# Two more gated channel pairs by seven block products, and the recurrence's chunks regrouped

## The chip, the cores and the metric

One core of a Trainium2 chip runs the whole program. The metric is the device time of one execution in microseconds (us); three runs of the kernel before have a median of 1548.71 us. TensorE (PE) multiplies matrices, ScalarE (ACT) applies functions and copies, VectorE (DVE) does elementwise arithmetic and scans, GpSimd (POOL) and SyncE (SP) mainly start transfers (DMA). Each engine works through its own instructions in the order in which the program lists them; between engines only semaphores order the work.

## What is computed

A decoder layer on `x` of 1024 positions by 1024 channels, all in float32:

```python
h = rms_norm(x, g_mix)
z = einsum("bsd,de->bse", h, w_in) + b_in
va, ga, xb, gb, sa, sb = split(z, cuts)      # 1024, 1024, 1536, 1536, 1024, 1024 channels
u = causal_depthwise_conv(va * sigmoid(ga), conv_a_w, conv_a_b)     # 31 taps
y_a = silu(layer_norm(u, ln_g, ln_b)) @ w_a_out
v = causal_depthwise_conv(xb, conv_b_w, conv_b_b)                   # 4 taps
r, i = sigmoid(block_diag(v, w_a) + b_a), sigmoid(block_diag(v, w_x) + b_x)   # 16 heads
a = exp(-8 * r * softplus(-lam))
hidden = scan(a, sqrt(1 - a*a) * i * v)      # linear recurrence over positions
y_b = (hidden * gelu(gb)) @ w_b_out
x = x + (sigmoid(sa) * y_a + sigmoid(sb) * y_b) @ w_o
x = x + square(relu(rms_norm(x, g_mlp) @ w_1)) @ w_2
out = rms_norm(x, g_final)
```

## The kernel before, in words

**Precision.** Every float32 operand is split into a high and a low part; a product is three matmuls (high by high, high by low, low by high). One matmul is a 128x128 weight block by 128x512.

**Columns of z.** They are numbered in chunks of 128 channels: VA 0 to 7, GA 8 to 15, XB 16 to 27, GB 28 to 39, SA 40 to 47, SB 48 to 55.

**First part** (the loop over `s`, one chunk a slot, order in the list `CH`). A chunk is 24 weight blocks by two halves of 512 positions, 48 matmuls (`chunk_mm`, line 735). The first part computes all of VA, GA and XB, 28 chunks. A VA/GA pair becomes `u = va*sigmoid(ga)` (`u_out`), and DVE runs the 31 taps on it (`conv`, lines 630 to 655, one filter of 48 instructions for each j). These taps are filler: a planner with a clock for each engine (`clk`, `later`, `vector_work`, `fill`) puts them between DVE's other work at build time. An XB chunk gets its four taps (`xb_out`) and is split (`xb_parts`); three XB chunks make a group of four heads. A head's two gates share one PSUM region of two banks (`ps2`, a single buffer): `head_mm(n, 0)` ends slot HS0[n], `head_gate(n, 0)` (a sigmoid on ACT, line 542) empties it, `head_mm(n, 1)` follows in the next slot behind 18 of the chunk's 24 blocks, `head_gate(n, 1)` empties it, and then comes `head_mm(n+1, 0)`. HS0 begins the four groups at slots 4, 9, 14 and 19, so that one slot without a new head lies between two groups. In the slot behind a group's last head comes `scan_exp` (three exp and three tanh on ACT), later `scan_root` (three square roots, line 564; `lag` puts it one slot further for the first three groups) and `scan_tile` for each of the group's three chunks (DVE, lines 573 to 576).

On ACT a slot's order is: `head_gate(before, 0)`, `xb_out` or `u_out`, `w_parts` (weights of the next chunk, two instructions), `head_gate(before, 1)`, `xb_parts`, `head_w_parts`, then `scan_exp` and `scan_root`. ACT holds one set of functions at a time; sigmoid, exp/tanh, and square root come with an ACT_TABLE_LOAD between them in the trace.

**Second part** (the loop over `zseq`). GB, SA and SB are computed by pairs of chunks: the weights as 2x2 blocks (two chunks by two halves of the 1024 input channels), the activations as 2x2 blocks (two halves of the channels by two halves of the positions), seven block products of 12 matmuls each (`z_mm`, line 933) in place of eight. `zseq` lists the products as (pair, p). Products 1, 2 and 3 take blocks of h as they are; 4 to 7 take sums and differences of them, which `x_load`, `x_sum` and `x_parts` prepare at the end of the first part and the start of the second. At step n of the loop: ACT copies or evacuates what product n-1 left (`z_post`), PE runs product n, ACT and POOL split the weight operand of product n+4 (`z_lhs`: either two ACT instructions with an accumulating POOL transfer between, or ACT and DVE), DVE makes the weight sums of product n+5 (`z_sums`), and SP starts loads listed in `ZL`. Product 1 of a pair fills PSUM bank a; `z_post` copies a to bank b, product 2 goes on accumulating in a, product 6 in b; b is copied to e and to a buffer u, product 7 fills f. A bank that no matmul has written before is first opened by one throwaway matmul (`z_bank`, line 922).

**After that** come the branch outputs (from line 1121), the layer norm of the filtered branch (it needs `ysum`, the sum of all eight filters' results), the output projection, and the MLP, all on PE.

The activation pool (`T`) has 37 tiles of 128x1024.

Of the kernel before, what the change touches and what calls it, by code (L numbers as in the profile page):

```python
# [9 lines left out]
F32 = mybir.dt.float32  # L10
# [3 lines left out]
ALU = mybir.AluOpType  # L14

P = 128
# [15 lines left out]
def trunk_kernel(ctx: ExitStack, tc: tile.TileContext, x, xt_in, xt_eo, vecs, w_in, w_a_out, w_b_out,  # L32
# [636 lines left out]
    def x_load(c2):  # L669

        xq[c2] = {n: ep.tile([P, S], F32, tag="e", name=f"xs{n}_{c2}") if (n, c2) == (21, 0) else T(f"xs{n}_{c2}")
                  for n in (11, 12, 22, 21)}
        for n, a in xq[c2].items():
            nc.sync.dma_start(a, xu[n % 10 - 1, 2 * (n // 10 - 1) + c2])
# [18 lines left out]

    CH = [XB, VA, GA, XB + 1, XB + 2]
    for js, g in (((1,), 1), ((2,), 2), ((3,), 3), ((4, 5, 6, 7), 4)):
        CH += [c for j in js for c in (VA + j, GA + j)]
        CH += [XB + t for t in range(3 * g, min(3 * g + 3, 12))]
    NC1 = len(CH)
# [39 lines left out]

    ZPAIRS = [GB + 2 * i for i in range(6)] + [SA + 2 * i for i in range(4)]
    ZPAIRS += [SB + 2 * i for i in range(4)]  # L740
    NZ = len(ZPAIRS)
# [3 lines left out]
    def z_load(i, kk):  # L745

        zraw[i, kk] = raw = qp.tile([P, 2, 4, P], F32, tag="p", name=f"zw{i}_{kk}", bufs=4)
        c = ZPAIRS[i]
        nc.sync.dma_start(raw, w_in[c:c + 2, :, 4 * kk:4 * kk + 4, :].rearrange("m p k c -> p m k c"))

# [18 lines left out]
    def z_lhs(i, p):  # L769
        src = z_blk(i, *{1: (0, 0), 2: (0, 1), 4: (1, 1)}[p]) if p in (1, 2, 4) else \  # L770
            zs[i, {3: 4, 5: 1, 6: 2, 7: 3}[p]]
# [12 lines left out]

    zseq = [(0, 1), (1, 1), (0, 2), (1, 2), (0, 6), (0, 7), (1, 7), (0, 5), (1, 6), (0, 3), (0, 4),
            (1, 5)]
    for i in range(2, NZ):
        zseq += [(i, 1), (i, 7), (i - 1, 4), (i, 6), (i, 2), (i - 1, 3), (i, 5)]
    zseq[-7:] = [(NZ - 1, p) for p in (1, 7, 6)] + [(NZ - 2, 4), (NZ - 1, 2), (NZ - 1, 5), (NZ - 2, 3)]
# [3 lines left out]
    for i in range(2, NZ):  # L793
        n = zseq.index((i, 1))
        ZL[n - 9] = ((z_load, i, 0),)
        ZL[n - (6 if i > 2 else 4)] = ((z_load, i, 1),)
    def z_get(n, f):
# [3 lines left out]
               mybir.EngineType.SP, mybir.EngineType.Pool}  # L801
    HS0 = [4 + 5 * (n // 4) + n % 4 for n in range(NH)]
    head_at = {s: n for n, s in enumerate(HS0)}

    EXP = {head_slot: g for g, head_slot in enumerate(HS0[4 * g + 3] + 1 for g in range(4))}
    XL = {23: 0, 25: 1}
    XS = {25: ((x_parts, 0, 6),), 26: ((x_parts, 0, 7, 5),), 27: ((x_parts, 0, 4),)}
    w_load(3)
# [5 lines left out]
    with tc.manual_schedule(engines=ENGINES):  # L814
        for s in range(3, NC1):
# [49 lines left out]
            for d in range(6):  # L865
                if s - d in EXP:
                    g = EXP[s - d]
                    lag = int(g < 3)
                    if d == 0:
# [48 lines left out]
    def z_bank(i, b):  # L918
        zb[i, b] = t = zp.tile([P, HS], F32, tag="z", name=f"z{i}{b}")
        if i < 2 and b in "be":  # L920

            nc.tensor.matmul(t, xh[0][0][:, 0:P], xh[0][0][:, 0:HS], start=True, stop=True)
        return t
# [14 lines left out]
    def z_out(i, m_, hf, src, name):  # L938
        ci = ZPAIRS[i] + m_
        bias = bin_c[:, ci:ci + 1]  # L940
        if ci < SA:
            t = ci - GB
# [9 lines left out]
        else:  # L952
# [5 lines left out]
            nc.sync.dma_start(halved(spill[b, j], hf), g)  # L958

    hb = {}  # L960

    def z_h(i, m_, hf):
        t = ZPAIRS[i] + m_ - GB
        if t < 12:
            hb[t, hf] = h = EV(f"hb{t}_{hf}")
            nc.sync.dma_start(h, hd[t, :, HALVES[hf]])
# [29 lines left out]

    ZX = {0: ((x_parts, 1, 7),), 7: ((later, 0, 4.8, scan_tile, 11),), 2: ((x_parts, 1, 5),), 4: ((x_parts, 1, 4),)}
    H_AT = {2: (0, 0), 5: (1, 1), 3: (0, 1), 4: (1, 0)}
    with tc.manual_schedule(engines=ENGINES):
# [19 lines left out]
        def hg_parts(*ts):  # L1019
            for t in ts:  # L1020
# [1085 lines left out]
```

## Time and profile before

| | us |
|---|---|
| median of 3 runs (lowest, highest) | 1548.71 (1548.26, 1549.64) |
| profiled execution, its own time | 1549.04 |
| its span, first to last instruction | 1547.2 |

| engine | busy us | share of span | instructions |
|---|---|---|---|
| PE (matmul) | 1535.6 | 99% | 6804 |
| DVE | 1214.5 | 78% | 1641 |
| ACT | 903.6 | 58% | 1266 |
| POOL | 188.6 | 12% | 226 |

The profile is of one execution. The 1.84 us between span and time lie outside the first and last instruction. Rows of a timeline give start, duration, engine, line, operation and operands; matmuls overlap in PE's pipeline, so their pace is read from the distance between starts, and not from the duration of one. The granted TensorE clock was 0.998 over the span. The first part's last matmuls start at 360.3 us, the second part's first at 360.57.

### The profile page before, as it was taken

Reading aid. Unit: us, or ns where it says so; the run is one execution under the profiler, and the core shown is the slowest. Engines: PE = TensorE matmul, PEld = TensorE weight load, DVE = VectorE, ACT = ScalarE, POOL = GpSimd, SP = SyncE. Lnnn points to the kernel's source line nnn. Section 1 sums busy time; section 2 is a strip of 40 time slices with the busy share of each in tenths; the row PEclk is TensorE's granted clock in tenths of the full one; section 3 lists DMA queues with packets and bytes.
Section 4 is the critical chain, followed back from the end, with each engine's and each line's share of the span. In section 5 each row is a group of like instructions: output and inputs, shape, how many; then the busy total and the mean of one; then the engine's idle time right before and its main releaser. Section 6 shows DMA issues by size and latency. Waiting matters only on the chain. (4 is left out here: it accounts for less than half of the span.)

```text
span 1547.2 us, 19086 instructions
## 1 busy us (share of the span) xinstructions
PE 1535.6 (99%) x6804; PEld 1264.6 (82%) x6804; DVE 1214.5 (78%) x1641; ACT 903.6 (58%) x1266; POOL 188.6 (12%) x226
## 2 busy tenths in 40 slices
PE   9999999999999999999999999999999999999998
PEld 7878888788888888888888887888888888888886
DVE  6999989999899983468568868765555558888897
ACT  6748677576667667435375777545444475555553
POOL 0000000002222222000022322000000001111110
PEclk9999999999999999999999999999999999999999
DMA  8653554678999889854579978523333779888852
GB/s 348 169 127 95 160 140 134 158 227 214 264 267 256 195 206 259 270 196 126 185 195 306 194 171 198 211 75 124 113 115 111 242 216 229 226 223 223 205 124 109
DMA packets 124943, 294.18 MB, mean 190 GB/s; under 512 B 12464, under 2 KB 30512, under 8 KB 124848
## 3 DMA queue, kind: packets, MB, share of 16 engines
q1 hardware_dynamic: 93312, 213.00, 40.7%
q0 software_dynamic: 31392, 79.71, 28.1%
q8 instruction: 53, 0.87, 0.2%
q14 instruction: 42, 0.34, 0.1%
q10 hardware_dynamic: 144, 0.26, 0.1%
HBM read 152.93 MB, written 58.72 MB: 137 GB/s over the span
## 5 line engine op out<-in xcount | busy, mean ns | idle before, releaser
L735 PE MATMUL z<-xh,win_h 128*128 128x512 f32 x400 | 125.0, 390 | 0.0
L735 PE MATMUL z<-xl,win_h 128*128 128x512 f32 x400 | 123.5, 390 | 0.0
L1873 DVE TENSOR_TENSOR acc<-acc,d 128x1024 f32<-128x1024 f32 x72 | 87.8, 1220 | 33.4 <-PE d L1861 32.7
L735 PE MATMUL z<-xh,win_l 128*128 128x512 f32 x400 | 99.4, 391 | 0.0
L735 PEld LDWEIGHTS z<-xh,win_l 128*128 128x128 f32 x400 | 75.2, 188 | 16.8
L735 PEld LDWEIGHTS z<-xh,win_h 128*128 128x128 f32 x400 | 75.1, 188 | 16.5 <-ACT win_h L68 0.4
L648 DVE SCALAR_TENSOR_TENSOR y<-u,vec,y 128x511 f32<-128x511 f32 (+14 forms) x120 | 88.5, 737 | 0.0
L735 PEld LDWEIGHTS z<-xl,win_h 128*128 128x128 f32 x400 | 75.1, 188 | 15.8
L648 DVE SCALAR_TENSOR_TENSOR yt<-u,vec,yt 128x511 f32<-128x511 f32 (+6 forms) x112 | 82.6, 737 | 0.0
L648 DVE SCALAR_TENSOR_TENSOR y<-yt,csum,y 128x511 f32<-128x511 f32 (+6 forms) x112 | 82.6, 737 | 0.0
L542 ACT ACTIVATE g<-rg,vec 96x1024 f32<-96x1024 f32 x32 | 35.6, 1113 | 79.6 <-PE rg L532 79.6
L1540 ACT ACTIVATE o<-s 128x512 fp32r<-128x512 f32 x58 | 34.7, 623 | 52.8 <-DVE s L1525 31.3
L67 POOL DMA_DIRECT2D win_l<-win_raw x25 | 21.6, 865 | 319.1 <-ACT win_l L66 248.4
L476 DVE SCALAR_TENSOR_TENSOR v<-xb,vec,v 128x1023 f32<-128x1023 f32 (+2 forms) x36 | 46.2, 1282 | 11.4 <-ACT v L467 10.4
L67 POOL DMA_DIRECT2D zo<-zw x42 | 36.2, 862 | 133.6 <-ACT zo L66 125.3
L1121 PE MATMUL yb<-hgl,wb_h 128*128 128x512 f32 x168 | 51.8, 390 | 0.0
L1121 PE MATMUL yb<-hgh,wb_h 128*128 128x512 f32 x168 | 51.8, 389 | 0.0
L66 ACT ACTIVATE zo<-zw 128x512 fp32r<-128x512 f32 x42 | 26.3, 626 | 30.7 <-DMA zw<-in_w_in_dram 8.7
L67 POOL DMA_DIRECT2D db_1l<-wr x7 | 6.0, 860 | 309.8 <-DMA wr<-in_w_dram 254.0
L1121 PE MATMUL yb<-hgh,wb_l 128*128 128x512 f32 x168 | 41.0, 390 | 0.0
L1085 DVE TENSOR_TENSOR o<-s,o 128x512 fp32r<-128x512 f32 x58 | 38.8, 682 | 0.0
L1121 PEld LDWEIGHTS yb<-hgh,wb_h 128*128 128x128 f32 x168 | 31.6, 188 | 6.5
(1795 smaller groups left out, 4672.9 us busy)
## 6 DMA issues: line engine op xcount, KB each, us to landing
w_raw<-in_w_dram SPq DMA_DIRECT2D x36, 512.0 KB, 5.5
fr<-fd SPq DMA_DIRECT2D x32, 512.0 KB, 5.9
wr<-in_w_dram SPq DMA_DIRECT2D x32, 512.0 KB, 6.5
zw<-in_w_in_dram SPq DMA_DIRECT2D x28, 512.0 KB, 5.9
win_raw<-in_w_in_dram SPq DMA_DIRECT2D x25, 512.0 KB, 4.1
win_l<-win_raw POOLq DMA_DIRECT2D x25, 512.0 KB, 4.5
zo<-zw POOLq DMA_DIRECT2D x42, 256.0 KB, 5.6
gates<-zg SPq DMA_DIRECT2D x32, 256.0 KB, 4.0
```

The lines of the kernel that those rows point to most:

```text
L66: nc.scalar.activation(l, src, AF.Copy, scale=-1.0)
L67: nc.gpsimd.dma_start(l, src, accum_op=ALU.add)
L476: nc.vector.scalar_tensor_tensor(v[:, d:S], a[:, 0:S - d], cbw_c[:, w * 12 + t:w * 12 + t + 1], v[:, d:S], ALU.mult, ALU.add)
L542: nc.scalar.activation(a, gps.pop((n, gi))[:HD, :], AF.Sigmoid, bias=(ba_c, bx_c)[gi][:, n:n + 1])
L648: nc.vector.scalar_tensor_tensor(o[:, k:], a[:, 0:HS - k], c, o[:, k:], ALU.mult, add)
L735: nc.tensor.matmul(zps[s][:, HALVES[hf]], w[:, k, :], xw[k][part][hf], start=n == 0, stop=n == 23)
L1085: tt(l, src, h.bitcast(F32), ALU.subtract)
L1121: nc.tensor.matmul(ps[hf], a, b[:, HALVES[hf]], start=n == 0, stop=n == len(todo) - 1)
L1540: nc.scalar.activation(o[:, 0], src, AF.Copy)
L1873: tt(acc[p, q2], acc[p, q2], ps, ALU.add)
```

## The change

The last two VA/GA pairs (j = 6 and 7) leave the first part, which then has 24 chunks, and become pairs 0 and 1 of the second part, in front of the 14 pairs that were there. `z_branch` is the new evacuation: it writes `u` by halves of the positions, value half 0 by ACT, the rest by DVE. The second part now begins with products 1 and 2 of pairs 0 to 3 (`FIRST = 4`; pairs 2 and 3 get their first blocks by separate loads, `z_first`), and the four throwaway matmuls now open bank b of pairs 0 to 3, in place of b and e of pairs 0 and 1. The XB chunks of the second and third group stand in a row, HS0 begins the groups at 4, 9, 13 and 17, and `lag` is 0 for all groups. `x_load`, `x_parts` and the last scans (chunks 10 and 11) move to later steps.

```diff
-        xq[c2] = {n: ep.tile(...) if (n, c2) == (21, 0) else T(f"xs{n}_{c2}")
+        xq[c2] = {n: ep.tile(...) if (n, c2) == (22, 0) else T(f"xs{n}_{c2}")
...
-    CH = [XB, VA, GA, XB + 1, XB + 2]
-    for js, g in (((1,), 1), ((2,), 2), ((3,), 3), ((4, 5, 6, 7), 4)):
-        CH += [c for j in js for c in (VA + j, GA + j)]
-        CH += [XB + t for t in range(3 * g, min(3 * g + 3, 12))]
+    NJ = 6
+    CH = [XB + 0, VA + 0, GA + 0, XB + 1, XB + 2, VA + 1, GA + 1, XB + 3, XB + 4, XB + 5, XB + 6, XB + 7, XB + 8, VA + 2, GA + 2, XB + 9, XB + 10, XB + 11, VA + 3, GA + 3, VA + 4, GA + 4, VA + 5, GA + 5]
...
-    ZPAIRS = [GB + 2 * i for i in range(6)] + [SA + 2 * i for i in range(4)]
-    ZPAIRS += [SB + 2 * i for i in range(4)]
+    ZPAIRS = [(VA + j, GA + j) for j in range(NJ, 8)]
+    ZPAIRS += [(c, c + 1) for c in range(GB, SB + 8, 2)]
...
+    def z_first(i):
+        for kk in range(2):
+            zraw[i, 0, kk] = raw = sp_.tile([P, HS], F32, tag="s", name=f"zf{i}_{kk}").rearrange(
+                "p (k c) -> p k c", c=P)
+            nc.sync.dma_start(raw, w_in[ZPAIRS[i][0], :, 4 * kk:4 * kk + 4, :])
...
-    zseq = [(0, 1), (1, 1), (0, 2), (1, 2), (0, 6), (0, 7), (1, 7), (0, 5), (1, 6), (0, 3), (0, 4),
-            (1, 5)]
+    FIRST = 4
+    zseq = [(i, p) for g in ((0, 1), (2, 3)) for p in (1, 2) for i in g]
+    zseq += [(0, 6), (0, 7), (1, 7), (0, 5), (1, 6), (0, 3), (0, 4), (1, 5)]
     for i in range(2, NZ):
-        zseq += [(i, 1), (i, 7), (i - 1, 4), (i, 6), (i, 2), (i - 1, 3), (i, 5)]
+        zseq += [x for x in ((i, 1), (i, 7), (i - 1, 4), (i, 6), (i, 2), (i - 1, 3), (i, 5))
+                 if x not in zseq]
...
-        n = zseq.index((i, 1))
-        ZL[n - 9] = ((z_load, i, 0),)
-        ZL[n - (6 if i > 2 else 4)] = ((z_load, i, 1),)
+        n = zseq.index((i, 7)) - 1
+        a, b = {2: (8, 4), 3: (10, 6)}.get(i, (9, 6))
+        ZL[n - a] = ((z_load, i, 0),)
+        ZL[n - b] = ((z_load, i, 1),)
...
-    HS0 = [4 + 5 * (n // 4) + n % 4 for n in range(NH)]
+    HS0 = [(4, 9, 13, 17)[n // 4] + n % 4 for n in range(NH)]
...
-    XL = {23: 0, 25: 1}
-    XS = {25: ((x_parts, 0, 6),), 26: ((x_parts, 0, 7, 5),), 27: ((x_parts, 0, 4),)}
+    XL = {NC1 - 4: 0, NC1 - 2: 1}
+    XS = {NC1 - 1: ((x_parts, 0, 6),)}
...
-                    lag = int(g < 3)
+                    lag = 0
...
-                    if 3 * g <= t < 3 * g + 3 and t < 11:
+                    if 3 * g <= t < 3 * g + 3 and t < 10:
...
-        if i < 2 and b in "be":
+        if i < FIRST and b == "b":
...
+    def z_branch(ci, hf, src, bias):
+        j = ci % GA
+        if j not in zu:
+            zu[j] = T(f"u{j}")
+        d, g = halved(zu[j], hf), src.rearrange("p (n o) -> p o n", o=2)
+        if ci >= GA:
+            zg[j, hf] = g
+            nc.scalar.activation(src, src, AF.Sigmoid, bias=bias)
+            ready = at("A", 0.62)
+            if hf == 0:
+                later(ready, 0.63, nc.vector.tensor_tensor, d, d, g, ALU.mult)
+                z_joined(j)
+        elif hf == 0:
+            nc.scalar.activation(d, g, AF.Identity, bias=bias)
+            at("A", 0.62)
+        else:
+            later(0, 0.68, nc.vector.scalar_tensor_tensor, d, g, bias, zg.pop((j, hf)), ALU.add, ALU.mult)
+            z_joined(j)
...
-    ZX = {0: ((x_parts, 1, 7),), 7: ((later, 0, 4.8, scan_tile, 11),), 2: ((x_parts, 1, 5),), 4: ((x_parts, 1, 4),)}
+    ZX = {0: ((x_parts, 1, 6), (later, 0, 4.8, scan_tile, 10)), 2: ((x_parts, 0, 7), (later, 0, 4.8, scan_tile, 11)),
+          3: ((x_parts, 1, 7),), 6: ((x_parts, 0, 5),), 7: ((x_parts, 1, 5),), 9: ((x_parts, 0, 4),),
+          10: ((x_parts, 1, 4),)}
...
-        for n in range(6):
-            z_get(n, z_sums)
+        z_first(2)
+        z_first(3)
         vector_work(clk["V"])
         z_get(2, z_lhs)
         z_get(3, z_lhs)
-        u_out(7, zps[NC1 - 2], zps[NC1 - 1])
-        x_parts(1, 6)
+        u_out(NJ - 1, zps[NC1 - 2], zps[NC1 - 1])
...
-            if n > 0:
-                z_get(n + 5, z_sums)
+            z_get(n + 5, z_sums)
```

More of the change, by code (lines that the diff above doesn't have):

```diff
@@ L669, in x_load @@
     def x_load(c2):
-        xq[c2] = {n: ep.tile([P, S], F32, tag="e", name=f"xs{n}_{c2}") if (n, c2) == (21, 0) else T(f"xs{n}_{c2}")
+        xq[c2] = {n: ep.tile([P, S], F32, tag="e", name=f"xs{n}_{c2}") if (n, c2) == (22, 0) else T(f"xs{n}_{c2}")
                   for n in (11, 12, 22, 21)}
@@ L747, in z_load @@
         zraw[i, kk] = raw = qp.tile([P, 2, 4, P], F32, tag="p", name=f"zw{i}_{kk}", bufs=4)
-        c = ZPAIRS[i]
-        nc.sync.dma_start(raw, w_in[c:c + 2, :, 4 * kk:4 * kk + 4, :].rearrange("m p k c -> p m k c"))
+        c, d = ZPAIRS[i]
+        nc.sync.dma_start(raw, w_in[c:d + 1:d - c, :, 4 * kk:4 * kk + 4, :].rearrange("m p k c -> p m k c"))
+    def z_first(i):
[3 more added lines that the diff above has]
+            nc.sync.dma_start(raw, w_in[ZPAIRS[i][0], :, 4 * kk:4 * kk + 4, :])
     def z_blk(i, m_, kk):
@@ L769, in z_lhs @@
     def z_lhs(i, p):
-        src = z_blk(i, *{1: (0, 0), 2: (0, 1), 4: (1, 1)}[p]) if p in (1, 2, 4) else \
-            zs[i, {3: 4, 5: 1, 6: 2, 7: 3}[p]]
+        if p in (1, 2) and 2 <= i < FIRST:
+            src = zraw[i, 0, p - 1]
+        else:
+            src = z_blk(i, *{1: (0, 0), 2: (0, 1), 4: (1, 1)}[p]) if p in (1, 2, 4) else \
+                zs[i, {3: 4, 5: 1, 6: 2, 7: 3}[p]]
         zn[0] += 1
@@ L938, in z_out @@
     def z_out(i, m_, hf, src, name):
-        ci = ZPAIRS[i] + m_
+        ci = ZPAIRS[i][m_]
         bias = bin_c[:, ci:ci + 1]
-        if ci < SA:
+        if ci < XB:
+            z_branch(ci, hf, src, bias)
+        elif ci < SA:
             t = ci - GB
@@ L958, in z_out, with z_joined @@
             nc.sync.dma_start(halved(spill[b, j], hf), g)
+    zu, zg = {}, {}
+    def z_branch(ci, hf, src, bias):
[13 more added lines that the diff above has]
+            at("A", 0.62)
+        else:
+            later(0, 0.68, nc.vector.scalar_tensor_tensor, d, g, bias, zg.pop((j, hf)), ALU.add, ALU.mult)
+            z_joined(j)
+    def z_joined(j):
+        if j in ut:
+            fresh.append(j)
+        ut[j] = zu[j]
     hb = {}
     def z_h(i, m_, hf):
-        t = ZPAIRS[i] + m_ - GB
-        if t < 12:
+        t = ZPAIRS[i][m_] - GB
+        if 0 <= t < 12:
             hb[t, hf] = h = EV(f"hb{t}_{hf}")
```

## The prediction

> **What bounds the kernel now.** I read the page first, then PE's own waits, then the timelines of PE, ACT and DVE around the recurrence's slots and around 360 us, where the second part begins.
>
> ```profile
> span 1547.2 us, 19086 instructions
> PE 1535.6 (99%) x6804; PEld 1264.6 (82%) x6804; DVE 1214.5 (78%) x1641; ACT 903.6 (58%) x1266; POOL 188.6 (12%) x226
> PE 38%; ACT 0%; DVE 0%; issue 0%; DVEq 0%; ACTq 0%
> ...
> PE gu4a L1297 <- ACT u_late L1351: 1.6, 1, 1.6
> ```
>
> PE is busy 99% of the span and the chain that ended last consists of PE alone. The last row is from the list of waits: the longest single wait of PE late in the kernel is 1.6 us. So the time is PE's matmuls plus the few microseconds in which PE stands still. A matmul removed is time won in full, and a wait added is time lost in full, since nothing behind it has slack to give back. I therefore count matmuls first and then look for places where PE would have to wait.
>
> PE's pace, from the starts of neighbouring groups in PE's timeline:
>
> ```profile
> 346.06 3.79 PE L735 MATMUL z<-xh,win_l 128*128 128x512 f32 x16
> ...
> 356.94 3.79 PE L735 MATMUL z<-xh,win_l 128*128 128x512 f32 x16
> 360.57 0.39 PE L933 MATMUL z0a<-xh,zo 128*128 128x512 f32 x1
> ...
> 363.29 0.39 PE L922 MATMUL z0b<-xh 128*128 128x512 f32 x1
> 363.52 0.39 PE L933 MATMUL z1a<-xh,zo 128*128 128x512 f32 x1
> ```
>
> The last third of one chunk starts at 346.06 and that of the next at 356.94: a chunk of 48 matmuls costs 10.88 us, 0.227 each. A block product of 12 takes 360.57 to 363.29, 2.72 us, the same pace. A throwaway matmul takes 0.23.
>
> **What the change removes.** Four chunks go, 4 x 10.88 = 43.52 us; fourteen products come, 14 x 2.72 = 38.08. That is 24 matmuls, **5.44 us less**. The throwaways are four before and four after: nothing. If no wait were added the profiled time would be 1549.04 - 5.44 = 1543.6. The saving is 0.35% of the time, so a handful of waits of one or two microseconds decides. A measurement of this kernel tells about 0.2%, 3.1 us, from no change.
>
> **The recurrence: the square roots one slot earlier.** ACT before, in slots 9 to 11, and the heads' first matmuls on PE:
>
> ```profile
> 134.54 0.34 ACT L518 ACTIVATE rgh<-rraw 96x192 fp32r<-96x192 f32 x1
> 134.91 1.28 ACT L542 ACT_TABLE_LOAD   x1
> 136.20 1.11 ACT L542 ACTIVATE g<-rg,vec 96x1024 f32<-96x1024 f32 x1
> ...
> 141.40 1.09 ACT L542 ACTIVATE g<-rg,vec 96x1024 f32<-96x1024 f32 x1
> ...
> 144.96 1.28 ACT L564 ACT_TABLE_LOAD   x1
> 146.26 2.96 ACT L564 ACTIVATE g<-g 128x1024 f32<-128x1024 f32 x3
> 149.24 1.28 ACT L542 ACT_TABLE_LOAD   x1
> ...
> 139.74 0.40 PE L530 MATMUL rg<-vth,rgh 96*96 96x512 f32 x1
> 143.90 0.40 PE L530 MATMUL rg<-vth,rgh 96*96 96x512 f32 x1
> ...
> 153.47 0.40 PE L530 MATMUL rg<-vth,rgh 96*96 96x512 f32 x1
> ```
>
> The sigmoid at 136.20 is `head_gate(4, 0)`; it ends at 137.31 and frees the single PSUM region for `head_mm(4, 1)` at 139.74, 2.43 us early. With `lag` 0 the roots of the first group stand at the end of slot 9, behind the row at 134.54 and ahead of this sigmoid. From their load to the next load they take 149.24 - 144.96 = 4.28 us. The sigmoid moves to 140.48, ends at 141.59, and PE waits 1.85 us. Two more instructions of `xb_out` and two of `w_parts` lie between it and `head_gate(4, 1)`, 141.40 - 136.20 = 5.20 us from start to start, so the second sigmoid ends 5.20 + 1.09 = 6.29 behind the first one's start. PE, released 1.11 behind that start, reaches `head_mm(5, 0)` 143.90 - 139.74 = 4.16 later, at 5.27: it waits again, 1.02. **Slot 10: 2.9 us.** Behind PE's waiting matmul stand the rest of the chunk and all that follows; nothing covers it. By the same reckoning the roots of groups 2 and 3 push a sigmoid that has 4 us and 0.5 us of room: no wait.
>
> **The recurrence: groups 2 and 3 in a row.** Before, the slot behind a group's exps has no sigmoid at its head. Now slots 14 and 18 have one, since the heads follow without a gap. The exps of slot 13 before, and the price of a sigmoid behind a tanh:
>
> ```profile
> 180.94 0.40 PE L530 MATMUL rg<-vth,rgh 96*96 96x512 f32 x1
> ...
> 182.53 1.11 ACT L542 ACTIVATE g<-rg,vec 96x1024 f32<-96x1024 f32 x1 [4.29 <-PE rg L532]
> ...
> 191.80 1.15 ACT L557 ACTIVATE g<-g,sm 128x1024 f32<-128x1024 f32 x1
> ...
> 323.42 1.28 ACT L587 ACT_TABLE_LOAD   x1
> 324.71 1.12 ACT L587 ACTIVATE u<-z,vec 128x1024 f32<-128x1024 f32 x1
> ```
>
> `head_mm(7, 1)` starts at 180.94, its sigmoid at 182.53, and the last tanh ends at 192.95. A load and a sigmoid behind it end 1.29 + 1.11 + 0.02 later, at 195.37. The next head's second matmul stands 153.47 - 139.74 = 13.73 behind the one at 180.94, at 194.67. **Slot 14: 0.7 us.** Chunk 13 is then a VA chunk, which adds nothing on ACT, so no second wait. **Slot 18: 0.7, and 1.0 more**, since chunk 17 is XB and the reckoning of slot 10's second wait holds again. First part together: 2.9 + 0.7 + 1.7 = 5.3 us.
>
> The Trainium skill, "ScalarE: Activation LUTs", section "What ACT_TABLE_LOAD costs", puts a switch of sets at 1283 ns for the load and about 1380 ns of drain, 2.66 us in all. This trace has the load at 1.28 and the next function 0.01 behind it, with no drain between (134.91 to 136.20, 323.42 to 324.71). By the page's sum each of the three places (slots 10, 14 and 18) would have one switch at 2.66 in place of 1.29, an estimate of 4.1 us more wait in all; I go by the rows.
>
> **The start of the second part: DVE.** It now has scans 9, 10 and 11 and the second `x_sum` around the border, ahead of the weight sums for product (0, 6):
>
> ```profile
> 329.03 2.96 ACT L564 ACTIVATE g<-g 128x1024 f32<-128x1024 f32 x3
> 338.81 0.62 PE L735 MATMUL z<-xh,win_h 128*128 128x512 f32 x2
> ...
> 331.97 1.22 DVE L573 SCALAR_TENSOR_TENSOR g<-a,g 128x1024 f32<-128x1024 f32 x1
> 336.82 0.53 DVE L641 TENSOR_SCALAR y<-yt,csum,cab 128x512 f32<-128x512 f32 x1
> 337.92 1.22 DVE L453 TENSOR_TENSOR xs6l<-xs,xs6h 128x1024 fp32r<-128x1024 f32 x1
> 343.90 1.26 DVE L453 SCALAR_TENSOR_TENSOR u<-z,vec,u 128x1024 f32<-128x1024 f32 x1
> 345.08 5.00 DVE L453 TENSOR_TENSOR xs<-xs,xs 128x1024 f32<-128x1024 f32 x4
> 360.36 0.68 DVE L453 TENSOR_TENSOR zs<-zw,zw 128x512 f32<-128x512 f32 x1
> 361.69 0.68 DVE L453 TENSOR_TENSOR zs<-zw 128x512 f32<-128x512 f32 x1
> ...
> 363.47 0.62 ACT L66 ACTIVATE zo<-zs 128x512 fp32r<-128x512 f32 x1
> 363.99 0.61 ACT L68 ACTIVATE zo<-zs 128x512 fp32r<-128x512 f32 x1
> 365.46 0.58 ACT L971 ACTIVATE z0b<-z0a 128x512 f32<-128x512 f32 x1
> ```
>
> The order of the last group is the same as before up to its roots, with the first part ending two chunks after its exps in place of four: the first root ends at 330.0, 8.8 us ahead of 338.81, which is where the first part now ends (call it T0). From there DVE has, with no room for filler: scan 9 (331.97 to 336.82, 4.85), the four sums (5.0), a low part (1.22), u5 (1.26), scan 10 (4.85), a low part, scan 11, a low part, and the two weight sums (360.36 to 361.69, 1.33): 25.8 us, to T0 + 17.0. ACT's split of that sum for (0, 6) waits for it, and behind it in ACT's order stands the copy of bank a to b for pair 2, two instructions (0.52 apart) later: it ends at 17.0 + 0.1 + 1.04 + 0.58 = T0 + 18.7. Product (2, 2) goes on accumulating in that bank a and cannot start before. Its own place is six products and four throwaways in, 6 x 2.72 + 4 x 0.23 = T0 + 17.2. **Wait: 1.5 us**, between 0 and 4 as the scans' order or a filter step shifts DVE.
>
> **Further in.** The second half of pair 2's weights takes the buffer of pair 0, which frees one step later against its load than before.
>
> ```profile
> zo<-zs POOLq DMA_DIRECT2D x28, 256.0 KB, 6.9
> zw<-in_w_in_dram SPq DMA_DIRECT2D x28, 512.0 KB, 5.9
> ```
>
> From the split of (0, 4) at step 10: transfer with issue 6.9, load 5.9, sums 1.3, ACT and POOL's start 1.5, transfer 6.9 makes 22.5 us, against eight products, 21.8, to (2, 6) at step 18. ACT reaches that split up to 2 us into its step. So 0.7 to 2.7 by median transfers, 0 with quicker ones; (1, 4) stands one product closer behind (1, 5) than before and waits in the same stretch for a copy that is behind the same split. I take **1.5 us**, with 0 and 3 as ends. SP's later loads of pair 3 and the hidden state queue behind the blocked load; they have more than three steps.
>
> At nothing I cost: `z_first`, four loads of 256 KB that can start when the last chunk's high weights are done, 3.63 us ahead of T0, and are wanted 3 us behind it (if they came later, each microsecond would be one of PE's); and the later filters. DVE starts filter 2 three slots later and has some 20 us more to do in the second part (ten instructions of 0.68 for each pair, a scan), so that the filters end up to 20 us later than here:
>
> ```profile
> L655 DVE TENSOR_TENSOR y<-y,yt x8: 678/684/687, 107.1 to 575.5; 128x511 f32<-128x511 f32 x8
> L1159 ACT ACTIVATE ysumh<-ysum x1: 1044/1044/1044, 649.3 to 649.3; 128x1024 fp32r<-128x1024 f32 x1
> ```
>
> The last filter ends at 575.5 and its sum is read at 649.3: 74 us of cover.
>
> **The sum.** -5.44 + 5.3 + 1.5 + 1.5 = +2.9: 1551.9 against the profiled 1549.04. The median of the runs is 0.33 below the profiled execution, so **1551.6**, at the upper edge of what counts as no change. With the ends of the two uncertain waits the forecast's own range is 1548.6 to 1555.6.
>
> **Rivals.** (1) The second part's start stays covered: DVE does the weight sums of (0, 6) by T0 + 15.5, for instance because a scan falls behind them, and transfers are quicker than their medians. Then only the first part's waits are left, -5.44 + 5.3: 1548.6, no change. For it: the matmuls at 356.94, 360.57 and 363.29 follow each other without a gap, so PE ran through this border here. Against: the chain of 25.8 us has no gap in it.
>
> (2) On the other side, faster: the first part's waits do not come. It decides at `head_gate(4, 0)`: if what stands ahead of it grows by less than 2.43 us, PE sees nothing, and the margins of 0.7 in slots 14 and 18 are small enough for ACT to be a little earlier there. With the second part as forecast this is -5.44 + 3.0, 1546.3; with neither, 1543.3. Against: the roots with their load are 4.28 us and the order on ACT is fixed.
>
> (3) Slower still: tiles run out. By my count the exps of slot 17 find 35 of 37 activation tiles in use and need three, so the last waits for a scan's release; here the scan should be done 5 us earlier. If it is not, the sigmoid of slot 18 is later by up to a scan, 4.85: 1556.5.
>
> (4) ACT stands still behind each load for as long as the load takes, 1.28: one load more ahead of each of the three sigmoids makes 3.8 us more, 1555.4. The rows with 0.01 behind a load speak against it. This is the place of the drain in the Trainium skill's "ScalarE: Activation LUTs", cited above.
>
> That the products are not saved I give no chance: their number follows from the lists.
>
> **Chances.** Forecast 0.5, (1) 0.18, (2) 0.2, (3) 0.1, (4) 0.02. Faster by over 0.2% (below 1545.6) is most of (2) with a few hundredths of quicker transfers: 0.2. Within 0.2% is (1) and the lower part of the forecast, together 0.34. Slower (above 1551.8) is the rest, 0.46. The range of eight in ten leaves out the best of (2) and the upper end of (3): 1545.0 to 1556.0.
>
> **What would show it.** PE's count falls from 6804 to 6780. In PE's waits: on ACT's sigmoid, two in slot 10 (1.9 and 1.0), one in slot 14, two in slot 18; one on the copy to z2b; one on a transfer or f bank near z2b or z1f. The forecast is wrong if rows 4.28 us long stand ahead of `head_gate(4, 0)` and PE's `rg` matmuls still keep 13.73, or if the waits of PE total much over 9 us.

## The result and the profile after

The changed kernel takes **1561.05 us** (median of 4 runs, 1560.48 to 1561.83) against 1548.49 for the kernel before on the same chip (4 runs, 1548.25 to 1549.64): 1.0080 times the time, 95% interval 1.0063 to 1.0097. It is slower by 12.6 us. The forecast was 1551.6, its range ended at 1556.0. The profiled execution took 1560.48 us.

The first lines and the chain of the page of the changed kernel, and the list of PE's waits (what waited, for whom: total us, times, longest us):

```profile
span 1558.7 us, 19117 instructions
PE 1535.1 (98%) x6780; PEld 1261.2 (81%) x6780; DVE 1225.3 (79%) x1659; ACT 916.5 (59%) x1295; POOL 194.2 (12%) x232
...
PE 85%; DVE 8%; ACT 3%; issue 2%; DMA 1%; POOL 0%; DVEq 0%; SPq 0%; ACTq 0%; POOLq 0%
```

```profile
PE z1f L943 <- DVE zc L453: 6.9, 1, 6.9
PE rg L530 <- ACT g L542: 3.8, 4, 1.8
...
PE z2a L943 <- ACT z2b L1009: 1.5, 1, 1.5
PE z4a L943 <- DMA zo<-zw: 0.7, 1, 0.7
...
PE gu4a L1335 <- ACT u_late L1389: 0.2, 1, 0.2
```

The 24 matmuls are gone (6780), and the chain that ended last, before made of PE alone, now runs through DVE, ACT and transfers too. Four of the five waits foreseen in the recurrence (`rg`) and the one before product (2,2) (`z2a`) are there. So is one that nobody had down at this size: 6.9 us before product (1,4), which writes bank `z1f`.

The list of waits doesn't hold everything, so I used one more reckoning for every kernel below, on PE's timeline from 40 to 660 us: the distance from the start of one group of matmuls to the start of the next, less 0.2267 us (10.88 / 48) for each matmul, summed where it is over 0.1 us. I call this sum the lost starts. The kernel before loses 1.0 us. The changed kernel loses 19.3:

| place in the changed kernel | lost, us | forecast, us |
|---|---|---|
| slot 10, first wait for the sigmoid | 1.97 | 1.9 |
| slot 10, second wait for the sigmoid | 0 | 1.0 |
| slot 10, matmuls at half pace behind the first wait (0.72 in the head, 0.90 in the chunk) | 1.62 | none |
| slot 11, first matmul of a head | 0.63 | none |
| slot 14 | 0.76 | 0.7 |
| slot 18 (0.76, 0.99) | 1.75 | 1.7 |
| product (2,2) | 1.68 | 1.5 |
| product (1,4): wait 7.08, half pace behind it 2.09 | 9.17 | 1.5 |
| product (4,2), a transfer | 0.90 | none |
| small ones | 0.84 | none |

Here is the stretch with the big one, rows of SP, DVE, POOL and PE (start, duration, engine, line, what, and in brackets how long the engine stood idle before and on whom):

```profile
364.29 6.10 SPq L747 DMA_DIRECT2D zw<-in_w_in_dram  x3
...
367.77 0.69 DVE L453 TENSOR_TENSOR zs<-zw,zw 128x512 f32<-128x512 f32 x1 [6.00 <-DMA zw<-in_w_in_dram]
...
370.29 0.86 POOL L67 DMA_DIRECT2D zo<-zs  x1 [2.85 <-ACT zo L66]
...
378.33 0.69 DVE L453 TENSOR_TENSOR zs<-zw 128x512 f32<-128x512 f32 x1 [4.63 <-DMA zo<-zs]
...
379.60 0.68 DVE L453 TENSOR_TENSOR zc<-zc,z1f 128x512 f32<-128x512 f32 x1
...
380.34 0.79 PE L943 MATMUL z1f<-xs4h,zo 128*128 128x512 f32 x1 [6.92 <-DVE zc L453]
380.93 0.63 PE L943 MATMUL z1f<-xs4l,zo 128*128 128x512 f32 x1
381.36 1.05 PE L943 MATMUL z1f<-xs4h,zo 128*128 128x512 f32 x2
```

DVE stands still twice. First for 6.00 us: its weight sums for (2,6) wait for the second half of pair 2's weights, loaded only at 364.29 into the buffer that pair 0 had just freed. Then for 4.63: the sum for (3,7) waits for one of the four buffers for sums, held by a transfer that POOL started late because of the first stop. Behind that sum in DVE's order stands the addition that reads bank f of pair 1 (379.60). It needs none of this, but PE may not overwrite the bank before it. PE stands still from 373.3 to 380.34, and the matmuls that follow start 0.43 apart in place of 0.23.

### The profile page after: what moved, and what is told of

It reads as the page before. It is cut to its first block, busy times and chain, and to the rows that moved or that the text cites. A ratio compares the mean times of both kernels' runs of the same rounds, so it can differ in the third digit from the quotient of the medians.

```text
span 1558.7 us, 19117 instructions
## 1 busy us (share of the span) xinstructions
PE 1535.1 (98%) x6780; PEld 1261.2 (81%) x6780; DVE 1225.3 (79%) x1659; ACT 916.5 (59%) x1295; POOL 194.2 (12%) x232
## 4 chain that ended last, share of the span: by engine, by line
PE 85%; DVE 8%; ACT 3%; issue 2%; DMA 1%; POOL 0%; DVEq 0%; SPq 0%; ACTq 0%; POOLq 0%
PE d L1899 15%; PE yb L1159 8%; PE z L733 6%; PE e L2016 3%; PE keep L1899 2%; DVE y L648 2%; PE z L258 2%; DVE v L476 1%; DVE yt L648 1%; DMA zo<-zw 1%; PE rg L530 1%; PE rg L532 1%; PE rg L531 1%; DMA zo<-zs 1%; PE z1f L943 0%
## 5 line engine op out<-in xcount | busy, mean ns | idle before, releaser
L733 PE MATMUL z<-xh,win_h 128*128 128x512 f32 x336 | 105.1, 390 | 0.0
L733 PE MATMUL z<-xl,win_h 128*128 128x512 f32 x336 | 103.7, 389 | 0.0
L733 PE MATMUL z<-xh,win_l 128*128 128x512 f32 x336 | 85.0, 394 | 0.0
L733 PEld LDWEIGHTS z<-xh,win_l 128*128 128x128 f32 x336 | 63.9, 190 | 14.7
L733 PEld LDWEIGHTS z<-xh,win_h 128*128 128x128 f32 x336 | 63.0, 188 | 14.0 <-ACT win_h L68 0.4
L733 PEld LDWEIGHTS z<-xl,win_h 128*128 128x128 f32 x336 | 63.1, 188 | 13.3
L67 POOL DMA_DIRECT2D win_l<-win_raw x21 | 18.2, 867 | 293.3 <-ACT win_l L66 213.5
L67 POOL DMA_DIRECT2D zo<-zs x32 | 28.0, 875 | 75.4 <-ACT zo L66 67.7
```

The costliest lines, as they stand in the source:

```text
L67: nc.gpsimd.dma_start(l, src, accum_op=ALU.add)
L733: nc.tensor.matmul(zps[s][:, HALVES[hf]], w[:, k, :], xw[k][part][hf], start=n == 0, stop=n == 23)
```

## The experiments

My theory after the result (A): the loss is a row of separate late links, each at the place of the table, and the big one is DVE's order. Its rivals: full DMA queues, DVE with more work than time, waits that come back elsewhere when one is taken away. All times are medians; each ratio is to the kernel before run beside it, whose medians lie between 1547.87 and 1548.49.

| kernel | us | ratio, 95% interval | lost starts, us | profiled time less lost starts |
|---|---|---|---|---|
| before | 1548.49 | 1 | 1.0 | 1548.0 |
| changed | 1561.05 | 1.0080 (1.0063 to 1.0097) | 19.3 | 1541.2 |
| e1 sum behind | 1555.38 | 1.0043 (1.0030 to 1.0055) | 14.4 | 1541.2 |
| e2 own buffer | 1557.43 | 1.0056 (1.0043 to 1.0068) | 16.0 | 1541.4 |
| e3 roots later | 1556.29 | 1.0051 (1.0038 to 1.0065) | 14.8 | 1541.5 |
| e4 scan later | 1564.76 | 1.0104 (1.0090 to 1.0118) | 22.9 | 1541.5 |
| f1 own buffer, sum behind | 1551.98 | 1.0026 (1.0017 to 1.0035) | 10.6 | 1541.5 |
| e7 copy ahead | 1561.54 | 1.0085 (1.0072 to 1.0099) | 19.9 | 1542.0 |
| e5 split ahead | 1558.97 | 1.0069 (1.0056 to 1.0081) | 19.3 | 1541.9 |
| b1 before with lag 0 | 1560.75 | 1.0084 (1.0070 to 1.0098) | 15.9 | 1547.6 |
| f3 f1 and copy ahead | 1552.05 | 1.0027 (1.0016 to 1.0037) | 10.5 | 1541.4 |
| best3 | 1547.71 | 0.9998 (0.9989 to 1.0007) | 7.2 | 1540.9 |
| best5 | 1545.33 | 0.9981 (0.9972 to 0.9990) | 3.9 | 1541.2 |

The last column tests the whole reckoning. Its profiled time is that of the one execution whose trace was taken, which is not always the median (in b1 it was the slowest of four, 1563.48). It is 1541 to 1542 for all eleven kernels with the change and about 1548 for the two without: a lost start of PE is lost time one for one, and the rest of the change is worth 6 to 7 us. The forecast was 5.44. Most of the difference lies behind the stretch that is counted: PE's wait before `gu4a`, 1.6 us in the kernel before, is 0.1 to 0.5 in the eleven kernels. Why it is shorter there no run shows.

**e1: the sum for (3,7) behind DVE's other work of step 16.**

```diff
-            z_get(n + 5, z_sums)
+            if n != 16:
+                z_get(n + 5, z_sums)
...
             vector_work(clk["P"] - 0.3)
+            if n == 16:
+                z_get(n + 5, z_sums)
+                vector_work(clk["V"])
```

> Edit: at step 16 of the second part the weight sum for the product after next, (3,7), is put behind DVE's other work of that step instead of ahead of it. The changed kernel took 1561.05 us; in its trace PE waits 6.92 us for bank f of pair 1 (product (1,4)), on a DVE addition that stands behind this sum, which itself waits 4.63 us for a buffer. Theory A (order on DVE): the addition no longer waits for that buffer; the 6.9 us and the half-pace matmuls behind it (about 2.5 us) go, product (2,6) then waits about 2 us for its weights; 1553.5 to 1556. Rival B (the late load of pair 2's second half at 364.29 is what counts, not the order): product (2,6), which stands right beside (1,4), waits nearly as long for its weights; at most 2 us saved, 1559 to 1561.

1555.38: 5.7 us less, as theory A said, but its picture was incomplete. DVE's rows and PE's wait in this kernel:

```profile
368.04 0.69 DVE L453 TENSOR_TENSOR zs<-zw,zw 128x512 f32<-128x512 f32 x1 [6.31 <-DMA zw<-in_w_in_dram]
...
375.21 0.68 DVE L453 TENSOR_TENSOR zc<-zc,z1f 128x512 f32<-128x512 f32 x1
...
379.03 0.69 DVE L453 TENSOR_TENSOR zs<-zw 128x512 f32<-128x512 f32 x1 [1.95 <-DMA zo<-zs]
```

```profile
PE z1f L943 <- DVE zc L453: 2.6, 1, 2.6
```

The addition no longer stands behind the sum at 379.03. It still comes 7.2 us behind the first stop, which is DVE's work of that time without a gap, and PE still waits 2.6. (2,6), where I expected 2 us of wait, doesn't wait at all. Two causes in a row, then, and this edit took away the second.

**e2: a buffer of its own for the second half of pair 2's weights, loaded five steps earlier.**

```diff
-        zraw[i, kk] = raw = qp.tile([P, 2, 4, P], F32, tag="p", name=f"zw{i}_{kk}", bufs=4)
+        if (i, kk) == (2, 1):
+            raw = T("zw2_1").rearrange("p (m k c) -> p m k c", m=2, c=P)
+        else:
+            raw = qp.tile([P, 2, 4, P], F32, tag="p", name=f"zw{i}_{kk}", bufs=4)
+        zraw[i, kk] = raw
...
-        a, b = {2: (8, 4), 3: (10, 6)}.get(i, (9, 6))
+        a, b = {2: (8, 9), 3: (10, 6)}.get(i, (9, 6))
```

> Edit: the second half of pair 2's weights gets a tile of its own instead of the buffer that pair 0 frees, and is loaded five steps earlier (step 5 instead of 10 counted in the list of loads). Theory A (the chain split of (0,4), transfer, load, sums, split, transfer is too long): the load is no longer behind the split of (0,4); DVE's sums of pair 2 come early, no sum waits for a buffer, PE's 6.9 us and the half pace behind it (2.5) go: 1551 to 1553.5. Rival C (DVE or the DMA queues are simply full in this stretch): the sums come no earlier than 4 us before, PE still waits 3 us or more near bank f of pair 1 or for the weights of (2,6): 1556 to 1560.

1557.43: 3.6 us less. The time and PE's wait of 3.6 us lie in rival C's range, but the sums come 6 us earlier, which rival C excluded. DVE's rows:

```profile
361.72 0.69 DVE L453 TENSOR_TENSOR zs<-zw,zw 128x512 f32<-128x512 f32 x1
...
365.82 0.75 DVE L453 SCALAR_TENSOR_TENSOR u<-z0e,vec,zc 128x512 f32<-128x512 f32 x1 [2.69 <-ACT zc L985]
...
375.02 0.69 DVE L453 TENSOR_TENSOR zs<-zw 128x512 f32<-128x512 f32 x1 [4.37 <-DMA zo<-zs]
...
376.30 0.68 DVE L453 TENSOR_TENSOR zc<-zc,z1f 128x512 f32<-128x512 f32 x1
```

The sums come at 361.72 in place of 367.77, without a wait for the load. But the sum for (3,7) still waits 4.37 us for a buffer with the addition behind it, so theory A's "no sum waits for a buffer" was wrong. This edit took away the first cause alone. (DVE now stops instead for ACT's sigmoid of the new evacuation, 2.69 us at 365.82; that one PE doesn't feel.)

**f1: the edits of e1 and e2 together.**

> Edit: the last two edits that helped, together: a tile of its own and an early load for the second half of pair 2's weights, and the sum for (3,7) behind DVE's other work of step 16. Measured before this run: the changed kernel 1561.05, the sum moved 1555.38 (its trace still has a wait of 2.56 us on the addition to bank f of pair 1, and 1.7 us of half-pace matmuls behind it), the own tile 1557.43 (3.59 and 1.6). Theory A (two causes in a row on DVE: the late load stops DVE for 6 us, the wait for a sums buffer for 4.6 more): with both gone the addition is done before PE asks for it, and the half pace goes: 1555.4 - 4.4 = 1551.0, to 1552. Rival G (DVE simply has more work here than time, about 7 us of instructions between the sums and the addition): 2 us of wait or more stay, 1554 to 1556.

1551.98, 9.1 us less than the changed kernel, and no wait at `z1f`: theory A. The addition stands at 372.00, ahead of the sum, which waits for its buffer without anyone behind it:

```profile
372.00 0.68 DVE L453 TENSOR_TENSOR zc<-zc,z1f 128x512 f32<-128x512 f32 x1
...
375.05 0.69 DVE L453 TENSOR_TENSOR zs<-zw 128x512 f32<-128x512 f32 x1 [1.15 <-DMA zo<-zs]
```

So DVE has the time (rival G falls), and the 9.2 us of the table's biggest row are accounted for. Separately the two edits give 5.7 and 3.6 us, together 9.1.

**e3: the first group's square roots one slot later, as before the change.**

```diff
-                    lag = 0
+                    lag = int(g == 0)
```

> Edit: the square roots of the first group alone go back to one slot later (lag 1 for group 0, 0 for the others). Theory A: PE's waits of 1.81 and 0.74 us for the sigmoid in slot 10 go, and with them about 0.7 us of half-pace matmuls behind the first: 3.6 us less, 1557.4. Rival D (half pace there has another cause than the wait): only 2.6 to 2.9 us less, and a granted clock under 1 stays near 142 us. Rival E (the roots had room to lose later on): the wait comes back in slot 11 or 14, less than 1 us saved, 1560 to 1561.

1556.29, 4.8 us less: theory A, and more than it said. The wait and the half pace in slot 10 are gone (the second wait of 0.74 us that the expectation names is not in the trace of the changed kernel; what is lost there is half pace), and so is the 0.63 in slot 11, which I had not tied to the roots. The heads' operands there come by transfers from SP. In the changed kernel a transfer of the scan's output, which follows the roots in the program, stands ahead of them in SP's order and waits for the scan; here the first of them goes out 16 us earlier. Rows of the changed kernel, then of e3:

```profile
152.68 0.33 SPq L577 DMA_DIRECT2D hd<-g  x1
153.10 0.52 SPq L507 DMA_DIRECT2D vh<-vth  x1
...
161.75 0.45 PE L530 MATMUL rg<-vh,rgh 96*96 96x512 f32 x1 [0.42 <-issue]
```

```profile
136.74 0.53 SPq L507 DMA_DIRECT2D vh<-vth  x1
```

Lost starts fall by 4.5. No run changes SP's order alone.

**b1: that part of the change alone, in the kernel before.**

```diff
-                    lag = int(g < 3)
+                    lag = 0
```

> Edit: the kernel before with one part of the change alone, lag 0 for all groups (square roots one slot earlier). There it meets a sigmoid at the head of the next slot in three places, slots 10, 15 and 20, since each group leaves one slot without a new head. Theory A (the roots with their table load are 4.28 us ahead of a sigmoid with 2.43 us of room; 2.9 us for two waits a place, up to 3.6 with slower matmuls behind the first): 3 x 2.9 to 3 x 3.6 more than 1548.4, 1557.1 to 1559.2, with three waits of 1.8 and three of 0.8 us in PE's list. Rival J (the loss in slot 10 of the changed kernel comes from the regrouped chunks, not from the roots): 1548 to 1550.

1560.75: 12.9 us more than the kernel before beside it (1547.87), over the range of theory A (8.7 to 10.8). PE's first heads of slots 10, 15 and 20, and its pace behind the last (0.43 from start to start):

```profile
141.71 0.47 PE L530 MATMUL rg<-vth,rgh 96*96 96x512 f32 x1 [1.76 <-ACT g L542]
...
211.23 0.48 PE L530 MATMUL rg<-vth,rgh 96*96 96x512 f32 x1 [1.90 <-ACT g L542]
...
281.57 0.48 PE L530 MATMUL rg<-vth,rgh 96*96 96x512 f32 x1 [1.69 <-ACT g L542]
...
282.69 0.63 PE L531 MATMUL rg<-vth,rgl 96*96 96x512 f32 x1
283.12 0.63 PE L532 MATMUL rg<-vtl,rgh 96*96 96x512 f32 x1
```

Three places, three first waits of the size worked out (1.92, 2.05 and 1.85 from start to start): the term for the roots holds in another kernel. A second wait stands in slot 15 alone (0.98); in slots 10 and 20 PE ran at half pace instead (1.6 us lost each) and came when the sigmoid had ended. The three places make 10 us of lost starts; the rest turned up at places that I had not listed, a chunk's weights (1.1), product (0,2) (1.1), and transfers for pairs 0, 2 and 4 (2.9 with the matmuls behind them). Together that is more than 12.9, since the profiled execution was 2.7 us over the median.

**e4: scan 11 two steps later.**

```diff
-          2: ((x_parts, 0, 7), (later, 0, 4.8, scan_tile, 11)),
+          2: ((x_parts, 0, 7),), 4: ((later, 0, 4.8, scan_tile, 11),),
```

> Edit: the scan of chunk 11 is put in at step 4 of the second part instead of step 2. Theory A: DVE's chain ahead of the weight sums of (0,6) is 4.8 us shorter, ACT's copy for pair 2 is no longer late, PE's wait of 1.53 us before (2,2) goes: 1559.3. Rival F (the chain only moves): the scan then delays sums or bank additions of a few steps later, PE waits as long near 350 us or longer for bank f of pair 1 at 380 us: 1560.5 to 1564.

1564.76, 3.7 us *more*: rival F, and a little over its range. PE's wait before (2,2) is gone, but the scan's 4.8 us now stand ahead of other things. The wait at bank f has grown, and three new waits of 0.5 to 1.0 us stand at pairs 0 and 1. The two longest of these four:

```profile
PE z1f L943 <- DVE zc L453: 9.5, 1, 9.5
...
PE z1b L943 <- DMA zo<-zs: 1.0, 1, 1.0
```

**e7: the split of (0,6) on ACT behind the copy for pair 2, one step later.**

```diff
             z_get(n - 1, z_post)
+            if n == 5:
+                z_get(8, z_lhs)
...
-            z_get(n + 4, z_lhs)
+            if n != 4:
+                z_get(n + 4, z_lhs)
```

> Edit: ACT's split of the weights of (0,6) is put one step later, behind ACT's copy of bank a to b for pair 2. Theory A (the copy is late only because it stands in ACT's order behind a split that waits for DVE's sums): PE's wait of 1.53 us before (2,2) goes, the split starts when the sums are there, as before: 1.7 us less, 1559.3. Rival H (what is won is paid at (0,6), whose weights come by a transfer behind that split): the wait turns up there, 1560.5 to 1561.5.

1561.54, no gain, though the wait before (2,2) is gone as foreseen and (0,6) doesn't wait. What was won was lost at neither theory's place:

```profile
PE z1f L943 <- DVE zc L453: 9.0, 1, 9.0
```

The wait at bank f grew from 6.9 to 9.0. PE came to it 0.6 us earlier (its last matmuls ahead of it start at 372.40 in place of 373.03), and the addition that ends it came 1.5 us later (381.06 in place of 379.60), since the load and the transfer that DVE waits for ended later. DVE's work from 341 to 361 us stands as in the changed kernel, 0.3 to 0.4 us later: what PE wins here doesn't move the chain that ends the wait. In e3, where PE and this chain both came 4 us earlier, the gain went through, and the wait was 7.2.

**f3: that edit on f1, where the wait at bank f is gone.**

> Edit: the kernel with the own tile, the early load and the sum (3,7) moved back (measured 1551.98), and the split of (0,6) behind the copy for pair 2. Alone on the changed kernel that last edit took away PE's wait before (2,2) but gained nothing (1561.54 against 1561.05), and the wait on bank f of pair 1 grew from 6.92 to 9.00 us. Theory A (the wait on bank f ends at a moment set by loads and transfers, so whatever PE wins ahead of it is lost there; without that wait the win stays): the trace of the kernel at 1551.98 loses 1.31 us before (2,2), so 1550.6, and no wait on bank f. Rival H (the split one step later costs as much elsewhere): 1551.5 to 1552.5.

1552.05, again no gain: against theory A. The 1.3 us before (2,2) went, and 0.95 came up inside (1,4), this time for its own weights (a transfer behind ACT's split, which stands behind a sigmoid and its table load), and 0.3 more before (1,1). The next late link was 1 us behind the one removed.

**e5: in slots 13 and 17, the splits ahead of the second sigmoid.**

```diff
-            if before is not None:
+            ahead = s in EXP and nxt is not None
+            if before is not None and not ahead:
                 head_gate(before, 1, clk["P"] - 12 * MM)
...
                 head_w_parts(nxt)
+            if before is not None and ahead:
+                head_gate(before, 1, clk["P"] - 12 * MM)
```

> Edit: in a slot that ends with a group's exps and has a new head in the next (slots 13 and 17), the split of the XB chunk and of the next head's weights go ahead of the second sigmoid on ACT instead of behind it, into time in which ACT waits for PE. Theory A (slots 14 and 18 wait because exp and tanh end late): the exps start about 2 us earlier, PE's three waits for the sigmoid there (0.76, 0.76 and 0.99 us from start to start) go, or the last one in part: 1.5 to 2.5 less, 1558.5 to 1559.5. Rival I (the second sigmoid of slots 13 and 17 becomes late by what is put ahead of it): new waits in slots 13 and 17, 1561 or more.

1558.97, 2.1 us less by the medians, as theory A has it. The waits of slot 14 and the first of slot 18 are gone, the second of slot 18 stays at 0.88. That the time gains by it is not clear of the noise: these five runs go from 1556.10 to 1561.21, those of the changed kernel from 1560.48 to 1561.83. The profiled execution was the slowest of the five, and its lost starts (19.3) show no gain.

**best3: everything that took a wait away.** f1, e7, e3 and e5 in one kernel.

> Edit: all the edits that took a wait away, together: own tile and early load for pair 2, sum (3,7) moved back, split of (0,6) behind the copy, the first group's roots one slot later, and the splits of slots 13 and 17 ahead of the second sigmoid. Theory A (the losses are separate waits of PE and add up once the wait on bank f, which swallows what is won ahead of it, is gone): from 1551.98 the trace has 1.92 + 0.99 + 1.34 us to win in slots 10 and 11, 0.75 + 0.75 in slots 14 and 18, 1.31 before (2,2): 7.1 less, 1544.9, faster than the kernel before (1547.9). Rival K (what is won early is lost again further on, to a transfer or to DVE): 1547 or more.

1547.71: equal to the kernel before, 2.8 us short of theory A. Rows of ACT, PE and POOL where it fell short:

```profile
178.27 1.24 ACT L467 ACTIVATE v<-xb,vec 128x1024 f32<-128x1024 f32 x1 [2.35 <-DMA hd<-g]
...
185.91 0.47 PE L530 MATMUL rg<-vth,rgh 96*96 96x512 f32 x1 [0.81 <-ACT g L542]
...
393.65 1.23 POOL L609 DMA_DIRECT2D ysum<-yd  x1
395.69 0.87 POOL L67 DMA_DIRECT2D zo<-zw  x1 [0.80 <-ACT zo L66]
```

With the roots one slot later, the scan's output leaves its tile later, and ACT waits 2.35 us for that transfer in slot 13. The splits, now ahead of the second sigmoid, carry this on to it, and PE waits in slots 13 and 14 (1.02 and 0.85). And (4,2) waits 1.48 for a transfer that stands on POOL's queue behind one for the filters' sum.

**best5: those three places mended.**

```diff
+            ahead = s == 17
...
-            if n >= 20 and n % 6 == 2:
+            if (n >= 20 and n % 6 == 2 and n != 26) or n == 28:
...
-            z_get(n - 2, z_post2)
+            if n != 13:
+                z_get(n - 2, z_post2)
...
+            if n == 13:
+                z_get(11, z_post2)
```

> Edit: the kernel with all five edits (measured 1547.71, equal to the kernel before), mended where its trace still has waits: the splits go ahead of the second sigmoid in slot 17 alone (in slot 13, where ACT was held 2.35 us by a transfer of the scan's output, this brought waits of 1.02 and 0.85 us from start to start); at step 13 ACT's split of the weights of (1,4) goes ahead of the sigmoid of pair 0 with its table load (PE waited 1.12 us for the transfer behind that split); the transfer that adds a filter's result to the sum goes from step 26 to step 28, out of the way of the transfer for (4,2) on POOL's queue (1.48 us). Theory A (each of these waits is one late link): 1.0 + 1.1 + 1.5 less, 1544.1, 0.25% under the kernel before. Rival K (the transfers are slow since the queues are full, whatever is put ahead): the two waits for transfers stay or move, 1546 to 1547.5.

1545.33, under the kernel before by 0.19% (0.10 to 0.28%). PE's waits that are left in the stretch counted:

```profile
PE rg L530 <- ACT g L542: 1.3, 2, 0.7
...
PE z2f L950 <- DVE zc L453: 0.6, 1, 0.6
PE z3a L950 <- ACT z3b L1016: 0.4, 1, 0.4
```

Both waits for transfers are gone, so the queues were not too full (rival K); 1.4 us came up behind them (`z3a`, `z2f`). This is the change with its order mended. Not tried: the bank openings of the first four pairs without the rest of the change, and more buffers for sums.

## Why the prediction was wrong, point by point

**The bound and the saving** held: every lost start is lost time, and 6780 matmuls are left. By the last column the saving was 6 to 7 us, and the shorter wait before `gu4a` accounts for most of what goes beyond the 5.44.

**Slot 10** held in its first wait (1.97 for 1.85), and e3 and b1 show the cause. The rows of the changed kernel are those that the prediction built by hand, roots of 4.28 us with their load ahead of the sigmoid, which starts at 140.46 where 140.48 was worked out:

```profile
134.89 1.28 ACT L564 ACT_TABLE_LOAD   x1
136.18 2.97 ACT L564 ACTIVATE g<-g 128x1024 f32<-128x1024 f32 x3
139.17 1.28 ACT L542 ACT_TABLE_LOAD   x1
140.46 1.11 ACT L542 ACTIVATE g<-rg,vec 96x1024 f32<-96x1024 f32 x1
...
145.65 1.10 ACT L542 ACTIVATE g<-rg,vec 96x1024 f32<-96x1024 f32 x1
...
141.62 0.47 PE L530 MATMUL rg<-vth,rgh 96*96 96x512 f32 x1 [1.81 <-ACT g L542]
...
147.43 0.40 PE L530 MATMUL rg<-vth,rgh 96*96 96x512 f32 x1
```

The second wait (1.02) is not in this execution. The second sigmoid ended at 146.75, and PE, slowed by the half pace, came only at 147.43. In e1, where the pace stayed full in slot 10, it is there with 0.99 from start to start:

```profile
146.68 0.48 PE L530 MATMUL rg<-vth,rgh 96*96 96x512 f32 x1 [0.80 <-ACT g L542]
```

So the reckoning of ACT's order was right in both waits. The term was still too small, by 1.3 us: slots 10 and 11 lose 4.2 together for 2.9. They lose 4.2 in e1 too, without the half pace, since the first head of slot 11 starts when SP's late transfers have landed (161.75, in e1 161.61). What the term left out is that order on SP's queue, whose rows stand with e3.

**Slots 14 and 18** (0.76 for 0.7; 1.75 for 1.7) and **product (2,2)** (1.68 for 1.5) held in place and size. e5 shows the cause of the former. For (2,2) the copy was late as reasoned, since e7 removes the wait, and the three null or worse results around it show what the sum didn't say: the next late link is within a microsecond (f3), the gain doesn't move the chain to bank f (e7), or other links get later by the edit (e4).

**"Further in" is the step that failed.** I put 1.5 us there, with 3 as the upper end, and 9.17 were lost at (1,4). The prediction's own sign of error, waits of much over 9 us in all, came with it. The chain itself was right: a load behind the split of (0,4), then sums, split and transfer. I followed it to the one product that uses those weights, (2,6), which in the end doesn't wait. I said of (1,4) only that it waits for "a copy that is behind the same split". What was missing is what DVE does meanwhile. The load stops DVE, and with it everything behind in its order. Next comes a sum that needs one of four buffers, whose release hangs on the same chain. The addition to bank f, harmless by itself, stood behind both. f1 shows it: with both stops gone the addition is at 372.00, and 9.1 us are won.

**The clock** was not in the sum at all. Behind the waits of 1.97 and 7.08 us the matmuls ran at half pace, 1.62 and 2.09 us. The first cost nothing in the end, as slot 11 shows; the second went with its wait in f1.

**The filters** ended far later than reckoned, 85 us and not up to 20. Groups and rows of the changed kernel:

```profile
L655 DVE TENSOR_TENSOR y<-y,yt x8: 682/684/689, 107.1 to 660.4; 128x511 f32<-128x511 f32 x8
...
673.37 1.07 ACT L1197 ACTIVATE ysumh<-ysum 128x1024 fp32r<-128x1024 f32 x1 [11.07 <-DMA ysum<-yd]
674.47 1.23 DVE L1123 TENSOR_TENSOR ysuml<-ysum,ysumh 128x1024 fp32r<-128x1024 f32 x1 [10.43 <-ACT ysumh L1197]
...
682.04 0.40 PE L1188 MATMUL mu<-ysuml,onesr 128*128 128x512 f32 x1
```

The last filter's last steps start at 660.4 (before 575.5), the sum's low part is there at 675.7, and PE asks for it at 682.04. Nothing was lost, as I had said, but only 6.3 us are left; before, the low part was there at 651.6 and PE asked at 669.0, 17.4 us later. In best5 the last steps start at 645.2, so the waits of PE are not the main reason; what the filters wait for is not traced.

**The rivals.** (1) and (2) fall with the waits that came. (3), tiles running out, didn't happen in slot 17; a mild form of it shows in slot 13 once the roots are moved back (178.27 above). (4) falls: at 139.17 the load takes 1.28 us and the sigmoid starts 0.01 behind it. The Trainium skill's drain of about 1380 ns behind each load ("ScalarE: Activation LUTs", "What ACT_TABLE_LOAD costs") isn't in these rows either.

## What to carry to other kernels

When a load or a buffer comes late, don't follow the data to its user alone: list what stands behind the waiting instruction on its engine or its queue of transfers, and who waits for each of those, since an addition that needs nothing of it held the matmuls for 7 us here. On a kernel that PE fills to 99%, moving steps earlier spends slack that no busy share shows, and each microsecond removed uncovers the next late link; the sum of lost starts tells whether a gain is real, here to about a microsecond for thirteen kernels. A wait that another engine's chain ends swallows a gain of PE that doesn't move this chain, so it is to be removed first.

## What the hardware did that I had not expected

A standstill of PE under 2 us can halve the pace of the matmuls behind it. Windows of 14 us, columns: the window, its length, busy time (count) of PE, PEld, DVE, ACT and POOL, the granted TensorE clock, the share of the DMA queues and GB/s; first the changed kernel in slot 10 and around (1,4), then e1 in slot 10:

```profile
136.00:150.00 14.00, 12.19 (x47) 9.13 (x46) 11.97 (x16) 12.79 (x14) 0.86 (x1) 0.88 0.34 80
...
372.00:386.00 14.00, 7.08 (x23) 5.37 (x22) 7.42 (x13) 3.02 (x7) 0.20 (x1) 0.76 0.46 116
```

```profile
136.00:150.00 14.00, 11.44 (x50) 8.52 (x49) 11.97 (x16) 12.78 (x15) 0.86 (x1) 1.00 0.34 80
```

In the same place the clock fell to a mean of 0.88 in one kernel and not in the other, behind standstills of 1.97 and 1.93 us. It fell there in e7 and f3 too (1.91 and 1.92), and not in e2 and f1 (1.92 both). In b1 it fell behind 1.92 and 1.85 us and not behind 2.05. By the starts of the matmuls, the half pace in these five places began 0.7 to 1.5 us after PE had gone on, and lasted about 3.3 us. So length alone doesn't decide it at this size; behind 2.72 us (e1) and all longer ones (3.75 to 9.69) the pace was always halved, and the matmuls lost 1.4 us or more by it. The Trainium skill, "TensorE: Matmul & The Clock Gate", "Part 1: The HAM clock gate (the "warmup" mystery)", has half rate after at least one idle window of about 3.4 us, with windows that run freely. Windows that don't start with the wait would fit the chance seen here, but no run here shows where they lie, and the figure is too large for these waits: 1.85 us of standstill was enough.
